# A low-part pass of attention logits on all 128 rows instead of 64

## The chip, the cores and the metric

The kernel runs on one core of a Trainium2 chip. The metric is device time in microseconds (us) of one execution; the time before is 652.01 us, the median of three runs (650.62 to 652.3).

The engines are named as the profile names them: PE is TensorE's matmul, PEld its weight load, DVE is VectorE, ACT is ScalarE, POOL is GpSimd, SP is SyncE, which issues most of the transfers. PE, DVE, ACT and POOL each run their own instructions in order and wait for one another by semaphores.

## The reference, cut to what matters

The reference is one encoder layer on 512 tokens of 1024 channels: a mixer (eight state-space heads and eight attention heads side by side), a norm, a mixture of 16 experts of which each token uses two, and a second norm. The change lies in the attention heads. For each head `h` of 64 channels and each block of 128 queries it computes

```python
logits = jnp.einsum('bqhd,bkhd->bhqk', q[:, q0:q1], k[:, :q1]) * scale   # d = 64
logits = logits + fcum[:, :, q0:q1, None] - fcum[:, :, None, :q1]
logits = jnp.where(qpos >= kpos, logits, -jnp.inf)
probs = jax.nn.softmax(logits, axis=-1)
out = jnp.einsum('bhqk,bkhd->bqhd', probs, v[:, :q1])
```

So query block `t` (0 to 3) needs logits against the first 128 (t + 1) keys.

## The kernel before, in words

**Stages.** The first 178 us project the input and run the state-space scans. The attention heads follow, to about 272 us, woven with projections that they do not depend on. Then come the rest of the output projection (to about 303 us), the first norm and the router (to about 326 us), 16 experts, one after the other (to about 618 us), and the last norms.

**Exact products from parts.** PE multiplies numbers of a reduced format (fp32r). The kernel therefore splits each operand into a high part and a low part, whose sum is the number, and leaves out only the product low by low. Usually that takes three passes: high by high, high by low and low by high.

**The parts of q and k.** `qk_proj` (L651) makes these for a pair of heads: `proj_T` (L243) leaves 128 channels by 512 tokens in a PSUM bank of the tag `pj`, which has two banks; rows 0 to 63 belong to the pair's even head and rows 64 to 127 to the odd one. The first round (m = 0) is q, the second (m = 1) is k. For head j of the pair, `own` are its 64 rows and `other` the rows of its neighbour. A tile `both[j]` of 128 rows by 512 columns takes, for q, the high part in `own` (L669, ACT) and the low part in `other` (L672, DVE). For k it takes the high part in both (L669 and L671, ACT). One pass over 128 rows of these two thus adds q high by k high and q low by k high. The low part of k goes to a third tile, `kl` (L672, DVE): both heads of the pair share one tile of 512 columns, each with its own 64 rows. It is cut from a slab of 1024 columns, of which the second half stays unused (L666).

**The logits.** `head_S` (L687) computes one head's block t into a PSUM bank by three passes: L694 over 128 rows (q's tile by k's tile, n = 128 (t + 1) columns), L695 over the 64 rows `rows` (q high by k low, n columns), and L696, which adds the causal mask to the last 128 columns with a bfloat16 identity as weights. Then DVE subtracts and finds the maximum (L700), ACT takes the exponential (L703), and DVE or POOL scale (L705). `head_T` (L707) transposes and splits the probabilities, `head_PV` (L718) multiplies by v, and `head_close` (L728) adds and splits the output. There are 8 heads of 4 blocks, and so 32 calls of `head_S`.

**Order of work.** PE runs strictly in the order in which the program emits its instructions (`MANUAL`, L78). `heads()` (L740) is a generator that yields amounts of time, and `weave` (L866) puts that much work from a second stream, `fill_stream` (L840), between its steps: projections of the next pairs' q and k (L250), then the output projection (L809). The fill runs on when the heads end, until 303 us. The other engines' orders are laid out by a planner from estimated times; instructions may be moved ahead of earlier ones there. The slabs (`U`, L163) are a ring of 31 buffers of 1024 columns, shared by all phases; the expert weights stream into the same ring as it comes free.

**POOL in this stage.** It computes the low parts of weights (L234, L795) and scales the logits of blocks 0 and 1 (L705).

Of the kernel before, what the change touches and what calls it, by code (L numbers as in the profile page):

```python
# [16 lines left out]
P = 128  # L17
# [55 lines left out]
# whose down projections follow an expert's gate and up projections  # L73
DOWN = [[]] + [[e - 1] for e in range(1, NEXP - 3)] + [[NEXP - 4, NEXP - 3], [NEXP - 2], [NEXP - 1]]
# order of the steps of the last norms: of a tile's, or the last expert's
# [7 lines left out]
def hybrid_layer(ctx: ExitStack, tc: tile.TileContext, x, xT, wu, w16, bT, bz, bv, b16, cw, cb,  # L83
# [22 lines left out]
    # ---- constants that depend on shapes alone  # L106
# [10 lines left out]
    # strict[j, l] = 1 where j < l  # L117
# [10 lines left out]
    # -big above the diagonal (column > row), and below it  # L128
# [11 lines left out]
    def rsqrt(o, var, mult, add, eng=V):  # L140
        """o = (var * mult + add) ** -0.5 on [P, n]"""
        eng.tensor_scalar(o, var, mult, add, op0=OP.mult, op1=OP.add)
        G.tensor_tensor(o, o, mhalf[:, : o.shape[1]], op=OP.pow)
# [5 lines left out]
    # tokens' places with each expert (1 and up, 0 for none), and what an expert's list holds  # L149
    # of a token: its number (less BIG) in two parts and its weight in three, exact in bfloat16  # L150
# [8 lines left out]
    # slabs of 4 KB and of 1 KB a partition, shared by all phases  # L159
# [17 lines left out]
    # ---- x^T and the columns of w_in as exact pairs of float32r parts  # L177
# [7 lines left out]
    def first_x(q, n):  # L185
        """x^T of two blocks of channels, in n parts: first the loads, then the splits"""
        xr = U("xr")
        h_, l_ = (wide("x", n, NX) if 2 * q + i < NX else U(n, F32R) for i, n in enumerate(("xh", "xl")))
        for j in range(2):
            xh[2 * q + j], xl[2 * q + j] = h_[:, j * S:(j + 1) * S], l_[:, j * S:(j + 1) * S]  # L190
        src = xT[q * 256:(q + 1) * 256, :].rearrange("(k p) s -> p k s", p=P)
        for j in range(n):
            c_ = slice(j * 1024 // n, (j + 1) * 1024 // n)
            SY.dma_start(xr[:, c_].rearrange("p (k s) -> p k s", s=S), src[:, j * 2 // n:(j + 1) * 2 // n])
            yield
        for j in range(n):
            c_ = slice(j * 1024 // n, (j + 1) * 1024 // n)
            split(h_[:, c_], l_[:, c_], xr[:, c_])
            yield

    def first_w(u, q, n):
        """half of a unit's columns, likewise"""
        wr_ = U(f"wr{u}")
        h_, l_ = wide("wh", f"wh{u}", 4), wide("wl", f"wl{u}", 4)
        units.setdefault(u, []).append([t_.rearrange("p (k c) -> p k c", c=256) for t_ in (h_, l_)])
        for j in range(n):
            c_ = slice(j * 1024 // n, (j + 1) * 1024 // n)
            SY.dma_start(wr_[:, c_].rearrange("p (k c) -> p k c", c=256),
                         wu[u, :, 4 * q + j * 4 // n:4 * q + (j + 1) * 4 // n])
            yield  # L210
        for j in range(n):
            c_ = slice(j * 1024 // n, (j + 1) * 1024 // n)
            A.activation(h_[:, c_], wr_[:, c_], AF.Copy)
            for d_ in (slice(c_.start, c_.start + 512), slice(c_.start + 512, c_.stop)):
                if d_.start < c_.stop:
                    G.tensor_tensor(l_[:, d_], wr_[:, d_], h_[:, d_].bitcast(F32), op=OP.subtract)
            yield
# [23 lines left out]
    # The tensor engine runs in the order of emission. Work is written as generators that  # L241
    # yield the tensor engine's microseconds, so that independent streams can be woven.
    def proj_T(u, m, r):  # L243
        """r gets out[channel, token] of 128 channels of a unit"""
        pt = bank("pj", "pjT")
        i = 0
        for k in range(KC):
            h_, l_ = units[u][k // 4]
            for w_, x_ in ((h_, xh), (h_, xl), (l_, xh)):
                T.matmul(pt, lhsT=w_[:, k % 4, m * P:(m + 1) * P], rhs=x_[k], start=(i == 0), stop=(i == 23))  # L250
                i += 1
            yield 0.64
        r.append(pt)

    def proj_T2(u, r):
        """both halves of a unit together, block by block as these arrive"""
# [10 lines left out]
    def proj_R(u, t, r):  # L267
        """r gets out[token, 256 channels] for one tile of tokens"""
# [10 lines left out]
    # ---- the first loads, in the order of their use  # L279
# [9 lines left out]
    # ---- per-channel parameters  # L289
# [17 lines left out]
    # rows (chunk, head) of a 64-row table: which head, which chunk  # L307
# [3 lines left out]
    # triones[j, l] = 1 where j <= l  # L311
# [16 lines left out]
    # bias of the convolution's input: what all four taps add, and what the first  # L328
    # three tokens lack of it
# [16 lines left out]
    # ---- dt and the forget gates: [token, tile, (dt 8 | f 8)]  # L346
# [8 lines left out]
    def gates():  # L355
# [15 lines left out]
        # softplus(v) = max(v, 0) + log1p(exp(-|v|)); log1p(e) = 2 atanh(e / (2 + e))  # L371
# [13 lines left out]
        # decays: da = dt * a, a = -exp(a_log)  # L385
        V.scalar_tensor_tensor(da, sp[:, :, 0:8], -1.0, an[:, None, :].to_broadcast([P, NT, 8]), op0=OP.mult, op1=OP.mult)
        V.tensor_scalar(dth, sp[:, :, 0:8], 0.5, None, op0=OP.mult)
        # 8 log f of head h on 16 copies each
# [5 lines left out]
        # cumulative sums within 128-token chunks, and their totals  # L394
# [8 lines left out]
        # rows -8 F[s]: partition (a, h) holds head h  # L403
# [8 lines left out]
        # the chunks' cumulative sums as rows (chunk, head), spread over a group's heads  # L412
# [13 lines left out]
    # ---- state-space heads, one group of four heads at a time  # L426
# [6 lines left out]
    def conv2(in_, blk):  # L433
        """2 silu(conv(proj + bias)) of 128 channels: [channel, token]"""
# [12 lines left out]
    def tt4(o, a, sc4, op, eng=V):  # L447
        """o[p, 256] = a[p, 256] op sc4[p, head]"""
# [8 lines left out]
    def prep(g):  # L457
        """projections, convolution and operands of a group's scan"""
# [37 lines left out]
        # hi and lo parts side by side, so that one pass serves both  # L496
# [35 lines left out]
    def scan(g):  # L532
        """yields the time that the tensor engine may be given to other work"""
# [8 lines left out]
        def decay(c):  # L542
            # decay matrix times C B^T: [s, (head, l)]
# [27 lines left out]
        for c in range(NT):  # L571
# [37 lines left out]
            # 2 silu(z) y, normed over the group's channels  # L609
# [18 lines left out]
    # ---- attention  # L628
    # (a head's hi and lo parts of v lie side by side, and those of its q one over the other,
    # so that one pass serves both)  # L630
# [20 lines left out]
    def qk_proj(pr):  # L651
# [3 lines left out]
        for m in range(2):  # L655
# [10 lines left out]
            kl = halves("kl")[0] if m else None  # L666
            for j in range(2):
# [4 lines left out]
                V.scalar_tensor_tensor(kl[own] if m else both[j][other], pt[own], bcol[own], both[j][own].bitcast(F32),  # L672
# [14 lines left out]
    def head_S(hd, t):  # L687
        q_, k_, kl = qk[hd // 2]
        q_, k_ = q_[hd % 2], k_[hd % 2]
        rows = slice((hd % 2) * HD, (hd % 2 + 1) * HD)  # L690
# [4 lines left out]
        T.matmul(sc[:, :n], lhsT=q_[rows, tq], rhs=kl[rows, :n], start=False, stop=False)  # L695
        T.matmul(sc[:, tq], lhsT=identb, rhs=maskq, start=False, stop=True)  # L696
        # -logits, and minus their maximum
# [42 lines left out]
    def heads():  # L740
        """yields the time that the tensor engine may be given to other work"""
# [42 lines left out]
    # ---- output projection; the state-space half of it fills the end of the attention  # L784
# [32 lines left out]
    # ---- router on rows u before their norm: logits = rs (u g wr - mu 1 g wr) + (b wr + br)  # L817
# [19 lines left out]
    # ---- weaving  # L837
# [54 lines left out]
    # ---- expert weights stream in from here on  # L892
    raw = {}

    def pieces():
        """the experts' weights in the order of their use: (expert, piece)"""
# [32 lines left out]
    # ---- experts  # L929

    def seats_of(pool, place_, eng):
        """[token, seat] of an expert: 1 where the token has the seat"""
# [6 lines left out]
    def list_of(pool, se, entry_, tokens=True, weights=True):  # L939
        """numbers of the tokens in 128 seats (I32), and their weights"""  # L940
# [52 lines left out]
    def gate_up(e, xt_, tag="pj"):  # L993
        """r gets the activations; yields after pairs of pieces"""
# [62 lines left out]
    # ---- second norm: in steps that may be woven  # L1057
    def stats(pool, halves_):
        """mean and variance of rows given as two halves"""
# [6 lines left out]
    def final(pool, u, t, o, junk, eng=V, st=V):  # L1066
        """a tile's rows, normed: with statistics from the engine st"""
# [20 lines left out]
    def final_last(u, ul):  # L1088
        """the last expert's tokens, normed"""
# [17 lines left out]
    def ln2_rows():  # L1107
        """the second norm's gain and bias on all partitions: a half of one at each step"""
# [14 lines left out]
    # ---- first norm, router  # L1123
# [5 lines left out]
    # what column i must exceed column j by, or equal, to come before it in order of size: nothing if  # L1129
    # i < j, the least number if i > j; and i = j never does  # L1130
# [92 lines left out]
    def rows_(t_):  # L1223
        """[p, tile, row, column] as [p, (tile, row), column]"""
# [4 lines left out]
    def choose(t0, t1):  # L1229
        """groups and experts of some tiles' tokens"""  # L1230
# [4 lines left out]
        # rows of four: the groups, and each group's experts; how many columns come before each  # L1235
# [10 lines left out]
    def seat():  # L1246
        """tokens' places: how many before them chose the expert, plus one"""
# [7 lines left out]
    def weigh():  # L1255
        """weights of the two: w0 = 1 / (sum exp (g - max)) / (1 + exp(l1 - l0)), w1 = w0 exp(l1 - l0); over alpha"""
# [97 lines left out]
    # tokens of each expert  # L1354
# [35 lines left out]
    # all tokens are finished without the last expert's product, and its tokens then redone  # L1390
# [31 lines left out]
    # ---- tokens beyond the first 128 of an expert  # L1422
    cnt = nc.values_load(cnt_i[0:1, 0:1], min_val=0, max_val=S, skip_runtime_bounds_check_because="at most every token")
    with tc.If(cnt > P):
        with tc.tile_pool(name="ov", bufs=1) as ov:
            # (and the last expert's first 128, whose products the sums above took from PSUM)
# [108 lines left out]
```

## Time and profile before

| | before |
|---|---|
| median of three runs | 652.01 us |
| range of the runs | 650.62 to 652.3 us |
| span of the profiled execution | 649.7 us |
| PE busy | 586.1 us (90%) |
| DVE busy | 529.2 us (81%) |
| ACT busy | 415.5 us (64%) |
| POOL busy | 248.7 us (38%) |
| PE's share of the chain that ended last | 62% |

The span runs from the first to the last instruction of one profiled execution; no other time is recorded for that execution. The three timed runs lie 0.9 to 2.6 us above it. A busy share is an average over stages; the chain of work that ended last says which engine set the time at each moment. In the chain, a piece's time is only its part of the chain, from its release to the next piece's, so that overlapping passes are not counted twice. In the timeline, a pass's duration includes the time for which it overlaps the next one.

### The profile page before, as it was taken

The numbers are of one execution on the slowest core, as the hardware profiler recorded it, in microseconds if no ns is written. First come the engines' busy times: TensorE is split into PE (matmuls) and PEld (weight loads), VectorE is DVE, ScalarE is ACT, GpSimd is POOL, SyncE is SP. The second block draws the span as 40 slices with busy tenths as digits, with TensorE's granted clock in tenths as the row PEclk, the third lists the DMA queues.
The fourth block names the chain that finished last, engine by engine and source line by source line (L and its number), as shares of the span: only waits on it lengthen the run. The fifth ranks groups of instructions, "written<-read, shape, count | busy, mean of one in ns | idle before, by whom it ended". The sixth has DMA issues, their size and how long they took to land.

```text
span 649.7 us, 9097 instructions
## 1 busy us (share of the span) xinstructions
PE 586.1 (90%) x3007; PEld 477.0 (73%) x3007; DVE 529.2 (81%) x869; ACT 415.5 (64%) x629; POOL 248.7 (38%) x248
## 2 busy tenths in 40 slices
PE   5888996999999999999398999999999999999950
PEld 4677786888776767788277888888888888877830
DVE  3986789688658797765879999999999999999673
ACT  5443353443577875523267888888888888887770
POOL 6537623733452341015614223333333322310282
PEclk9897997999999999998589999999999999999985
DMA  8421122211111174994888999999999999992342
GB/s 263 137 74 54 65 66 66 82 66 64 66 66 45 47 238 134 369 370 165 307 293 307 320 371 358 382 361 352 346 350 341 366 343 361 322 361 55 115 176 83
DMA packets 61702, 141.39 MB, mean 218 GB/s; under 512 B 9987, under 2 KB 10003, under 8 KB 61648
## 3 DMA queue, kind: packets, MB, share of 16 engines
q1 hardware_dynamic: 55168, 125.79, 54.1%
q0 software_dynamic: 5904, 12.85, 7.1%
q10 hardware_dynamic: 576, 2.10, 0.8%
q8 instruction: 25, 0.41, 0.3%
q14 instruction: 29, 0.24, 0.1%
HBM read 134.69 MB, written 14.68 MB: 230 GB/s over the span
## 4 chain that ended last, share of the span: by engine, by line
PE 62%; DVE 13%; ACT 6%; issue 6%; DMA 6%; POOL 5%; SPq 0%; POOLq 0%; ACTq 0%; DVEq 0%
PE pw L809 6%; PE pg L1003 5%; PE pg L1005 4%; PE pg L1004 4%; PE py L1037 4%; PE pu L1003 4%; PE pu L1005 4%; PE pu L1004 4%; PE py L1039 4%; PE py L1038 4%; PE pjT L250 4%; PE pjR L274 3%; DVE acc L437 3%; PE pxg L979 2%; DMA wr<-in_wu 1%
## 5 line engine op out<-in xcount | busy, mean ns | idle before, releaser
L986 ACT ACTIVATE eh<-wf 128x1024 fp32r<-128x1024 f32 x192 | 203.1, 1061 | 49.8 <-PE pg L1005 15.2
L234 POOL TENSOR_TENSOR wl<-wr,wh 128x512 fp32r<-128x512 f32 x40 | 57.0, 1449 | 45.0 <-ACT wh L229 42.2
L957 POOL DMA_INDIRECT xg<-hb,ix x16 | 21.1, 1317 | 112.7 <-PE pg L1005 107.5
L1043 POOL DMA_INDIRECT ub<-yo,ix x15 | 27.2, 1811 | 88.7 <-ACT at L103 54.4
L1037 PE MATMUL py<-eh,at 128*128 128x512 f32 x128 | 52.5, 410 | 2.7 <-ACT at L103 2.5
L1003 PE MATMUL pg<-eh,xgh 128*128 128x512 f32 x128 | 53.1, 415 | 0.8 <-ACT xgh L103 0.8
L1039 PE MATMUL py<-eh,at 128*128 128x512 f32 x128 | 50.9, 398 | 0.0
L1005 PE MATMUL pg<-eh,xgl 128*128 128x512 f32 x128 | 50.7, 396 | 0.0
L1003 PE MATMUL pu<-eh,xgh 128*128 128x512 f32 x128 | 50.0, 391 | 0.0
L1005 PE MATMUL pu<-eh,xgl 128*128 128x512 f32 x128 | 49.9, 390 | 0.0
L250 PE MATMUL pjT<-xh,wh 128*128 128x512 f32 x112 | 46.3, 413 | 1.6 <-DVE kl L672 1.6
L274 PE MATMUL pjR<-wh,xh 128*128 128x256 f32 x128 | 39.3, 307 | 8.6 <-ACT acc L429 7.6
L250 PE MATMUL pjT<-xh,wl 128*128 128x512 f32 x112 | 44.1, 394 | 0.0
L250 PE MATMUL pjT<-xl,wh 128*128 128x512 f32 x112 | 43.9, 392 | 0.0
L936 POOL TENSOR_SCALAR se<-seats,place 128x128 bf16<-128x128 f32 x56 | 43.5, 792 | 0.5
L274 PE MATMUL pjR<-wl,xh 128*128 128x256 f32 x128 | 38.1, 298 | 0.0
L274 PE MATMUL pjR<-wh,xl 128*128 128x256 f32 x128 | 38.0, 297 | 0.0
L274 PEld LDWEIGHTS pjR<-wh,xh 128*128 128x128 f32 x128 | 26.3, 206 | 9.3 <-ACT acc L429 8.0
L1037 PEld LDWEIGHTS py<-eh,at 128*128 128x128 f32 x128 | 24.5, 191 | 8.6 <-ACT at L103 2.7
L1005 PEld LDWEIGHTS pg<-eh,xgl 128*128 128x128 f32 x128 | 24.3, 190 | 6.1 <-DVE xgl L104 0.8
L1039 PEld LDWEIGHTS py<-eh,at 128*128 128x128 f32 x128 | 24.4, 191 | 5.9 <-DVE at L104 0.8
L1003 PEld LDWEIGHTS pg<-eh,xgh 128*128 128x128 f32 x128 | 24.3, 190 | 5.0 <-ACT xgh L103 1.2
(951 smaller groups left out, 1757.7 us busy)
## 6 DMA issues: line engine op xcount, KB each, us to landing
wf<-in_w_up SPq DMA_DIRECT2D x64, 512.0 KB
wf<-in_w_gate SPq DMA_DIRECT2D x64, 512.0 KB
wf<-in_w_down SPq DMA_DIRECT2D x60, 512.0 KB
wr<-in_wu SPq DMA_DIRECT2D x22, 512.0 KB
wor<-in_w_out SPq DMA_DIRECT2D x8, 512.0 KB
hh<-in_x SPq DMA_DIRECT2D x4, 512.0 KB
wf<-in_w_down POOLq DMA_DIRECT2D x4, 512.0 KB, 7.9
u<-ub SPq DMA_DIRECT2D x4, 512.0 KB
```

What stands on the lines that cost most here:

```text
L234: G.tensor_tensor(l_[:, j], wr_[:, j], h_[:, j].bitcast(F32), op=OP.subtract)
L250: T.matmul(pt, lhsT=w_[:, k % 4, m * P:(m + 1) * P], rhs=x_[k], start=(i == 0), stop=(i == 23))
L274: T.matmul(pt, lhsT=x_[k][:, t * P:(t + 1) * P], rhs=w_[:, k % 4, :], start=(i == 0), stop=(i == 23))
L809: T.matmul(pw, lhsT=m_[k][:, ts_], rhs=wo[k][w_][:, c_], start=(i == 0), stop=(i == 11))
L936: eng.tensor_scalar(r[t], seats, place_(t), None, op0=OP.is_equal)
L986: A.activation(h_, src, AF.Copy)
L1003: T.matmul(pt, lhsT=h_[:, k], rhs=wh_[:, f], start=(k == 0), stop=False)
L1004: T.matmul(pt, lhsT=h_[:, k], rhs=wl_[:, f], start=False, stop=False)
L1005: T.matmul(pt, lhsT=l_[:, k], rhs=wh_[:, f], start=False, stop=(k == KC - 1))
L1037: T.matmul(pt, lhsT=h_[:, f], rhs=wh_[:, c_], start=(f == 0), stop=False)
L1039: T.matmul(pt, lhsT=l_[:, f], rhs=wh_[:, c_], start=False, stop=(f == 3))
L1043: G.indirect_dma_start(out=ub, out_offset=bass.IndirectOffsetOnAxis(ap=ix, axis=0), in_=yo, in_offset=None, bounds_check=S - 1, oob_is_err ...
```

## The change

The tile `kl` becomes two, one for each head of the pair, in the two halves of the slab that was taken before too. In each, the head's `own` rows take the low part of k as before, and POOL writes zeros to the `other` rows. The second pass of `head_S` then uses all 128 rows of q's tile and of `kl[j]`: the rows of q low are multiplied by zeros. The rest of the diff removes comments, and moves no other instruction.

```diff
@@ qk_proj
-            kl = halves("kl")[0] if m else None
+            kl = halves("kl") if m else None
             for j in range(2):
                 own, other = slice(j * HD, (j + 1) * HD), slice((1 - j) * HD, (2 - j) * HD)
                 A.activation(both[j][own], pt[own], AF.Identity, bias=bcol[own])
                 if m:
                     A.activation(both[j][other], pt[own], AF.Identity, bias=bcol[own])
-                V.scalar_tensor_tensor(kl[own] if m else both[j][other], pt[own], bcol[own], both[j][own].bitcast(F32),
+                    G.memset(kl[j][other].bitcast(F32), 0.0)
+                V.scalar_tensor_tensor(kl[j][own] if m else both[j][other], pt[own], bcol[own], both[j][own].bitcast(F32),
                                        op0=OP.add, op1=OP.subtract)
@@ head_S
-        q_, k_ = q_[hd % 2], k_[hd % 2]
-        rows = slice((hd % 2) * HD, (hd % 2 + 1) * HD)
+        q_, k_, kl = q_[hd % 2], k_[hd % 2], kl[hd % 2]
...
         T.matmul(sc[:, :n], lhsT=q_[:, tq], rhs=k_[:, :n], start=True, stop=False)
-        T.matmul(sc[:, :n], lhsT=q_[rows, tq], rhs=kl[rows, :n], start=False, stop=False)
+        T.matmul(sc[:, :n], lhsT=q_[:, tq], rhs=kl[:, :n], start=False, stop=False)
         T.matmul(sc[:, tq], lhsT=identb, rhs=maskq, start=False, stop=True)
```

## Rows read from the trace of the kernel before

**Rows 1.** The page's head and its first part: busy us, share, instructions.

```profile
span 649.7 us, 9097 instructions
PE 586.1 (90%) x3007; PEld 477.0 (73%) x3007; DVE 529.2 (81%) x869; ACT 415.5 (64%) x629; POOL 248.7 (38%) x248
```

**Rows 2.** Stretches: PE, PEld, DVE, ACT, POOL busy (instructions), clock, DMA share, GB/s.

```profile
178.00:272.00 94.00, 91.02 (x452) 66.66 (x450) 68.76 (x183) 65.29 (x144) 29.08 (x27) 1.00 0.40 138
222.00:233.00 11.00, 10.95 (x56) 8.10 (x55) 8.45 (x21) 9.87 (x19) 6.89 (x4) 1.00 0.42 132
...
450.00:500.00 50.00, 50.00 (x249) 41.13 (x248) 47.97 (x59) 41.97 (x52) 17.44 (x16) 1.00 0.98 346
```

**Rows 3.** Line L695: idle us of PEld before it, times.

```profile
  issue: 7.9, 32
```

**Rows 4.** Chain that ended last, 257 to 273 us: start, us, piece.

```profile
257.02 0.06 PE sc L694
257.08 0.25 PE sc L695
257.33 0.16 PE sc L696
257.49 0.75 PE pw L809 x3
258.24 0.12 PE sc L694
258.36 0.31 PE sc L695
...
259.27 0.70 PE pw L809 x3
...
260.31 0.18 PE sc L694
260.48 0.36 PE sc L695
...
263.95 0.23 PE sc L694
264.18 0.43 PE sc L695
264.61 0.18 PE sc L696
...
271.74 0.41 PE po L725 x4
```

**Rows 5.** Timeline of PE, 64 to 65 us: start, duration, instruction.

```profile
64.21 0.73 PE L547 MATMUL pl<-RL,csel 64*128 64x512 f32 x2
64.87 0.39 PE L548 MATMUL pl<-maskl,identb 128*128 128x512 bf16 x1
```

**Rows 6.** POOL by line and form: busy us, mean ns.

```profile
L322 POOL MEMSET cself<- 64x512 f32 x1 | 0.5, 523 | 0.0
```

**Rows 7.** Timeline of POOL and PE, 170 to 182 us; brackets: idle before, releaser.

```profile
170.79 2.73 POOL L234 TENSOR_TENSOR wl<-wr,wh 128x512 fp32r<-128x512 f32 x2
...
175.38 0.47 PE L250 MATMUL pjT<-xh,wh 128*128 128x512 f32 x1 [1.58 <-DVE kl L672]
...
179.35 2.55 POOL L234 TENSOR_TENSOR wl<-wr,wh 128x512 fp32r<-128x512 f32 x2 [5.83 <-ACT wh L229]
```

**Rows 8.** Chain that ended last, 196 to 238 us, parts not on PE.

```profile
199.34 0.09 ACT lg L703
...
201.34 2.51 DVE m L104
...
205.04 0.50 PE po L725
...
218.63 0.69 DVE lg L700
...
236.09 0.77 DVE kl L672
```

## The prediction

> **What bounds the kernel now.** I read the page's shares first [rows 1]: PE is busy 90% of the span, DVE 81%, ACT 64%. Such averages do not price one stage, so I went to the stretch of the attention heads [rows 2]. Of its 94.0 us PE is busy 91.0, DVE 68.8 (73%), ACT 65.3 (69%) and POOL 29.1 (31%), at a granted clock of 1.00, the upper level of 2.4 GHz. PE has 3.0 us of idle time there, so what it saves should move the end, unless another engine is the limit in some part. Whether one is, the chain of waits tells, below.
>
> Next I looked at the pass that changes. Ahead of L695 the weight load sat idle 7.9 us in 32 times, 0.25 us each, and for nothing that a semaphore shows ("issue") [rows 3]. So the weights of the 64-row pass are not loaded while the pass before it runs, as they are elsewhere. The chain of one head's four calls shows what that costs [rows 4]. L694, over 128 rows, takes 0.06, 0.12, 0.18 and 0.23 us of the chain for 128, 256, 384 and 512 columns. L695, over 64 rows and as many columns, takes 0.25, 0.31, 0.36 and 0.43: a nearly constant 0.18 to 0.20 more. The same excess stands at the only other 64-row pair [rows 5]: two L547 passes of 512 columns start at 64.21 and the next pass at 64.87, 0.66 us for both. Plain passes of 512 columns take 0.23 (0.70 for three at 259.27 [rows 4]), and 0.66 is 0.23 + 0.43. So two 64-row passes in a row pay the excess once: it belongs to leaving that form, and not to the pass.
>
> **The change part by part.** *The 32 passes (PE).* Before, in the chain, with the mask pass L696 and what the three plain passes behind take beyond 0.70 (0.75 at 257.49, so 0.05) [rows 4]: 128 columns 0.06 + 0.25 + 0.16 + 0.05 = 0.52; 256 columns 0.12 + 0.31 + 0.16 = 0.59 (transposes follow; the 0.16 of L696 repeats for 256 and 384); 384 columns 0.18 + 0.36 + 0.16 + 0.05 = 0.75; 512 columns 0.23 + 0.43 + 0.18 + 0.05 = 0.89.
>
> After, L695 is a pass as L694 is. The price of a short one comes from four plain passes at the end of the heads, two of 256 columns and two of 128, 0.41 us in all [rows 4]: 0.12 + 0.12 leaves 0.17 for the two short ones, 0.06 and 0.11, the second held up by the next weights. So 128 columns: 0.11 + 0.06 and 0.12 for the mask pass with the load behind it, 0.29. 256 columns: 0.12 + 0.12 + 0.07 = 0.31. 384 columns: 0.18 + 0.18 + 0.12 = 0.48. 512 columns: 0.23 + 0.23 + 0.12 = 0.58. The saving is 0.23 + 0.28 + 0.27 + 0.31 = 1.09 us a head, 8.7 us for eight. From below: if only L695 itself becomes plain and the mask pass keeps its price, 0.14 + 0.19 + 0.18 + 0.20 = 0.71 a head, 5.7 us. From above, the mask pass at 0.06 and nothing behind it: 0.06 more in three of the four calls, 10.2 us. I take 8.7, since the idle weight loads of [rows 3], 7.9 us, and some idle ahead of the mask's weights agree with it.
>
> The Trainium skill speaks against this. "TensorE: Matmul & The Clock Gate", section "LDWEIGHTS (loading the stationary operand)", has the time of a weight load depend on the columns alone, so that a load of few rows takes as long as one of 128. By that rule the row count would be worth nothing, and the sum 0. The same skill, in "TensorEngine Tiling (Array Packing)", section "Key Properties", says that a change of the tiling mode drains the engine. By that one the excess goes with the mode. The trace sides with the second: 0.43 against 0.23 us for the same columns [rows 4], and 0.66 for two in one mode [rows 5].
>
> *Eight memsets (POOL).* The nearest row is a memset of the same shape, 0.523 us [rows 6]; 8 make 4.2 us. POOL is idle 65 of the 94 us [rows 2], and nothing has to be read, so that a memset can run as soon as its slab is free. With that cover it costs nothing; from above, if each stood in front of the chain, 4.2 us. I take 0, since kl of the first pair is ready at about 175.4, and the program lets L695 read it only after the projections and the head's opening; POOL has an idle stretch of 5.8 us just then, before 179.35 [rows 7].
>
> *The added wait.* L695 now waits for DVE and POOL. PE is in order, so everything of both streams stands behind it; it costs nothing while the zeros are ready before the low part. If the planner makes the DVE step of `kl` wait for the memset as well, behind it on DVE stand the softmax steps, and the PSUM bank that PE needs for its next projection: PE waited 1.58 us for exactly that release at 175.38 [rows 7]. Between 0 and the price of the slower rival below I take 0, as the two instructions write different rows.
>
> *What is late next.* Two parts of the heads' chain do not run on PE [rows 8]. From 199.34 to 205.04 it runs over ACT and DVE, with one subtraction of 2.51 us on DVE. From 218.63 to 236.09 it runs over ACT, POOL, a load of output weights and ACT again; ACT is busy 9.87 of 11 us there [rows 2]. What PE saves inside these stretches it then waits. A head lasts about (264.18 - 218.4) / 4 = 11.4 us (the last call of head 7 [rows 4] against that of head 3, just before DVE's 218.63 [rows 8]), so that 5.7 + 17.5 = 23.2 us hold two heads' worth of calls: 2.0 x 1.09 = 2.2 us lost. Between 0 lost (these stretches begin earlier and also get shorter) and 4.4 (twice as much), I take 2.2.
>
> *Behind the heads.* The output projection is PE's to 303 us and starts earlier. The norm and the router are a chain of latencies that moves as a whole. The experts keep PE busy 50.00 of 50 us [rows 2], so they end earlier by as much. Their weights are a stream of 0.98 DMA share; a lead of 6.5 us asks for 6.5 x 346 = 2.2 MB, some four or five slabs, sooner, and the heads free their slabs sooner by about the same time.
>
> *Sum.* 8.7 - 2.2 = 6.5 us. Against the profiled span: 649.7 - 6.5 = 643.2. The median of the runs stands 2.3 us above that span, and I leave the distance: 652.0 - 6.5 = 645.5 us.
>
> **The rivals.**
> *All of it is kept.* If the ACT stretches start earlier by what PE gained before and have slack, 8.7 us come through: 643.3. For it: ACT is busy only 69% over the stage. Against: it is nearly full just where the chain lies on it.
>
> *Another engine takes over.* With PE at 91.0 - 8.7 = 82.3 us, DVE's 68.8 and ACT's 65.3 come close, both wait on one another within each head, and new estimates may change the planner's order on ACT and DVE. Then only 2 to 4.5 us are left, 648.8 in the middle.
>
> *Nothing moves.* Either the row count is not the cause, as the skill's first rule would have it, or the weights' stream sets the end of the experts whatever comes before: 652.0. For the latter: a DMA share of 0.98. Against: PE does not pause in those 50 us, and it is PE that would wait if the stream were late.
>
> *Slower: the zeros hold up the low part of k.* The place is L672 at m = 1, once for each pair. If the dependence is kept for a tile and not for its rows, DVE's step waits for the memset, the memset for its turn on POOL behind the weight parts of the next unit, two of them 2.73 us at 170.79 [rows 7], and the second memset again for the first step on DVE: 2.73 + 2 x 0.52 = 3.8 us at worst for a pair, 15 for four. From 6.5 / 4 = 1.6 us a pair on it eats the gain; at 3 us a pair the time is 652.0 - 6.5 + 12 = 657.5. For it: PE already waits for `kl` at 175.38 [rows 7], and the chain passes through `kl` at 236.09 [rows 8]. Against: a memset reads nothing, and POOL has room.
>
> **How the numbers follow.** Forecast (645.5, its own range 643.8 to 647.5): 0.52. All kept: 0.15. Another engine takes over: 0.16. Nothing moves: 0.08. Slower: 0.09. The range leaves out the slower case, half of the unmoved one and the lower tail of the first rival: 642.6 to 651.5. 0.3%, 2.0 us, is about what a measurement of this kernel can tell from no change; by that, faster 0.82 (0.52 + 0.15 + most of 0.16), same 0.09, slower 0.09.
>
> **What would show it.** Right: L695's rows read 128*128; no "issue" idle stands ahead of its weight loads; in the chain a 512-column L695 takes 0.23; the last call of the heads starts 6 to 7 us earlier, and every expert starts earlier by the same. The loss would show as longer waits of PE at the passes behind 205 and 236 us, for DVE and ACT. Wrong: L695 keeps 0.43 (then rows are not the cause); POOL's memsets stand behind a weight part, and PE or DVE wait for them; or the heads end earlier but PE begins to wait within the experts for weights. The forecast is wrong on its size if PE's new waits in the heads add up to more than 5 us or less than 1.

## The result, and the profile after

| | before | changed |
|---|---|---|
| median | 652.15 us (650.62 to 652.45, 4 runs) | 646.05 us (645.41 to 646.51, 4 runs) |
| profiled execution | span 649.7 us | 646.35 us, span 644.3 us |
| heads: head 0's opening to the last mask pass | 178.34 to 264.54 us, 86.2 | 177.54 to 258.66 us, 81.1 |

The ratio of the times is 0.9909, with a 95% interval of 0.9886 to 0.9933: 6.1 us faster, and between 4.4 and 7.4. The forecast was 645.5 us.

In the changed kernel the lines have moved a little: the three passes of `head_S` are L695, L696 (the low part of k) and L697 (the mask), the memset is L673, the low part of k L674, the transposes are L716, the products with v L726, the output projection is L810, and its weights' low part L796. The page's head and first part answer to [rows 1] (busy us, share, instructions):

```profile
span 644.3 us, 9107 instructions
PE 577.7 (90%) x3007; PEld 476.5 (74%) x3007; DVE 529.4 (82%) x869; ACT 415.0 (64%) x629; POOL 252.7 (39%) x256
```

PE has as many instructions as before and is busy 586.1 - 577.7 = 8.4 us less; POOL has eight more instructions and 4.0 us more. The span is only 5.4 us shorter. The stretches, in the columns of [rows 2]:

```profile
178.00:266.00 88.00, 82.51 (x447) 65.12 (x445) 69.46 (x183) 64.18 (x144) 32.28 (x33) 1.00 0.44 146
222.00:233.00 11.00, 8.94 (x45) 6.30 (x43) 9.73 (x19) 9.03 (x18) 7.10 (x6) 1.00 0.71 239
450.00:500.00 50.00, 50.00 (x249) 41.13 (x248) 47.96 (x60) 42.17 (x52) 17.15 (x17) 1.00 0.98 348
214.00:235.00 21.00, 18.61 (x100) 14.17 (x99) 17.10 (x39) 18.00 (x36) 10.88 (x8) 1.00 0.46 151
```

In the heads PE is now idle 88.00 - 82.51 = 5.5 us, where it was idle 3.0 [rows 2]. Of the eleven microseconds from 222 it leaves 2.06 unused, where it left 0.05. In the experts nothing has changed: PE is full, and DMA has the same share. Next the line of the low part by itself, answering to [rows 3] (duration ns, least, median and most; first and last start; shapes):

```profile
L696 PEld LDWEIGHTS sc<-kl,qk x32: 187/188/192, 179.5 to 258.2; 128*128 128x128 f32 x32
L696 PE MATMUL sc<-kl,qk x32: 273/307/397, 179.5 to 258.4; 128*128 128x128 f32 x8, 128*128 128x256 f32 x8, 128*128 128x384 f32 x8, 128*128 128x512 f32 x8
its engine sat idle before it (us, times) until:
who waited for it (us, times):
```

Nothing stands under the idle time: the 7.9 us of issue are gone. The timeline of head 7's call of 512 columns (start, duration, instruction; in brackets idle before, releaser) shows where they stood, in the lines of PE and PEld. First the kernel before:

```profile
263.79 0.40 PE L694 MATMUL sc<-qk 128*128 128x512 f32 x1
264.11 0.18 PEld L695 LDWEIGHTS sc<-kl,qk 64*128 64x128 f32 x1 [0.36 <-issue]
264.11 0.50 PE L695 MATMUL sc<-kl,qk 64*128 64x512 f32 x1
...
264.54 0.23 PE L696 MATMUL sc<-maskq,identb 128*128 128x128 bf16 x1
```

Then the changed kernel:

```profile
258.19 0.40 PE L695 MATMUL sc<-qk 128*128 128x512 f32 x1
258.19 0.19 PEld L696 LDWEIGHTS sc<-kl,qk 128*128 128x128 f32 x1
258.42 0.40 PE L696 MATMUL sc<-kl,qk 128*128 128x512 f32 x1
...
258.66 0.23 PE L697 MATMUL sc<-maskq,identb 128*128 128x128 bf16 x1
```

The weights are now loaded at 258.19, a whole pass ahead, where the load stood until 264.11 before. From start to start, the pass ahead took 0.32 us and the 64-row pass 0.43; they take 0.23 and 0.24 now. So the form cost 0.09 on the way in and 0.19 on the way out. The chain of waits within head 1 (start, us, piece) gives the prices that answer to [rows 4]:

```profile
186.32 0.12 PE sc L695
186.44 0.12 PE sc L696
186.56 0.07 PE sc L697
186.63 0.37 PE ptr L716 x3
187.00 0.02 issue
187.02 0.33 PE ptr L716
```

L696 now takes what L695 takes, 0.12 us for 256 columns (the other calls, not shown, have 0.06 and 0.11 for 128 columns, twice 0.18 for 384 and twice 0.23 for 512), and the mask pass behind it 0.07 in place of 0.16. The four transposes after the second call are what went the other way. They took 0.44 us before and take 0.37 + 0.02 + 0.33 = 0.72: PE comes to the fourth one before DVE has scaled its block. DVE's timeline there (start, duration, instruction) shows what DVE was doing:

```profile
184.26 1.46 DVE L706 TENSOR_SCALAR lg<-lg,rs 128x384 f32<-128x384 f32 x1
...
186.48 0.49 DVE L706 TENSOR_SCALAR lg<-lg,rs 128x512 f32<-128x512 f32 x1
```

The scaling of 384 columns took 1.46 us, most of it beside a weight part on POOL (182.94 to 185.48). In the kernel before, the same scaling came at 186.13, after POOL's weight part had ended at 185.89, and took 0.44, although POOL ran a scaling beside it. The block that PE waits for was then ready at 187.82, 1.0 us before the transposes began (188.83); now it is ready at 186.97, and they begin at 186.47. Over the heads, the eight scalings of 384 columns take 695 ns on the mean, against 496 before.

PE's waits for other engines within the heads (engine, line, what it waited for: us in total, times, longest), 177 to 267 us:

```profile
PE po L726 <- DVE pl L104: 1.6, 1, 1.6
PE ptr L716 <- DVE lg L706: 1.2, 2, 0.7
PE po L726 <- DVE plq L104: 0.9, 1, 0.9
PE pw L810 <- DVE kl L674: 0.7, 1, 0.7
PE prq L832 <- DVE rq L829: 0.6, 1, 0.6
PE ptr L716 <- DVE pl L104: 0.4, 2, 0.2
```

These are 5.4 us in all. In the kernel before, the same answer over the heads has four lines of 1.0, 0.7, 0.7 and 0.5 us: po for DVE's pl, ptr for lg, pw for kl, prq for rq, 2.9 in all. The listed waits have grown by 2.5 us, all of it at DVE, as much as the idle time of the stretches. The chain where it leaves PE, answering to [rows 8]:

```profile
198.52 2.47 DVE m L104
...
203.59 1.06 ACT woh L795
...
209.19 0.76 DVE kl L674
```

It is off PE at the places of before, and also in between, from 203.59 to 213.20, where ACT copies output weights, makes the next q and k and takes exponentials. Last, POOL's timeline (start, duration, instruction), answering to [rows 7]:

```profile
170.43 1.09 POOL L673 MEMSET kl<- 64x512 f32 x2
171.49 2.51 POOL L234 TENSOR_TENSOR wl<-wr,wh 128x512 fp32r<-128x512 f32 x2
```

The two memsets of the first pair ran ahead of the weight parts and not behind them. Each took 0.52 us, and in all eight cases nobody waited for them, though a scaling of 384 columns on DVE that ran beside one took 0.76 us in place of 0.42 (at 202.70, and likewise at 206.23 with the zeros alone below). They did one thing that was not foreseen: they pushed the weight part behind a step of DVE that it had run beside. DVE's timeline there, in the kernel before (first line) and in the changed one:

```profile
170.87 1.50 DVE L616 SCALAR_TENSOR_TENSOR zs<-zs,rst,g_bz 128x256 f32<-128x256 f32 x1 [0.97 <-POOL rst L143]
170.40 0.48 DVE L616 SCALAR_TENSOR_TENSOR zs<-zs,rst,g_bz 128x256 f32<-128x256 f32 x1 [0.97 <-POOL rst L143]
```

`kl` follows on DVE, and PE's wait for it ahead of the heads, 1.58 us in [rows 7], is 1.25 now. Of the fourteen executions in this document, the three without memsets have 1.50 for this step and 1.58 or 1.59 for the wait. The eleven with them have 0.48 or 0.49, and waits of 1.25 to 1.27, but for the two that clear more rows (1.39 and 0.67).

**Where the time went, head by head.** I take the time from one head's opening (`pfb`) to the next one's. For head 7 the end is the start of its last mask pass. From head 0 to head 7 the gains are 1.07, 0.71, 0.56, 0.71, -0.22, 0.22, 0.94 and 1.09 us, 5.1 in sum. What a head saves without its waits is read from its four calls, each from the start of its first pass to the start of what follows its mask pass: head 7's took 0.44, 0.59, 0.76 and 0.79 us, and take 0.21, 0.30, 0.47 and 0.51. That is 1.09 less, and heads 0 and 7 bring all of it through. Eight times that is 8.7, near the 8.4 by which PE's busy time fell. Against 1.09 a head, heads 4 and 5 lost 2.2 us, head 2 lost 0.5, heads 1 and 3 lost 0.8 (0.28 of it at the transposes above), head 6 lost 0.1, and heads 0 and 7 nothing: 3.6 in all. The rest of the profiled difference lies outside the heads. The changed kernel's execution reached them 0.8 us sooner, 0.3 of it by the shorter wait for `kl`, and took 0.5 us longer behind them: 0.8 + 5.1 - 0.5 = 5.4. That start moved from 177.5 to 180.4 us over the executions below, in no order of their edits.

### The profile page after: what moved, and what is told of

Its sections match the earlier page's. It is cut to its first block, busy times and chain, and to the rows that moved or that the text cites. A ratio compares the mean times of both kernels' runs of the same rounds, so it can differ in the third digit from the quotient of the medians.

```text
span 644.3 us, 9107 instructions
## 1 busy us (share of the span) xinstructions
PE 577.7 (90%) x3007; PEld 476.5 (74%) x3007; DVE 529.4 (82%) x869; ACT 415.0 (64%) x629; POOL 252.7 (39%) x256
## 4 chain that ended last, share of the span: by engine, by line
PE 57%; DVE 15%; ACT 8%; DMA 7%; issue 6%; POOL 5%; SPq 0%; POOLq 0%; ACTq 0%; DVEq 0%
PE pw L810 6%; PE pg L1004 5%; PE pg L1006 4%; PE pg L1005 4%; PE py L1038 4%; PE pu L1004 4%; PE pu L1006 4%; PE pu L1005 4%; PE py L1040 4%; PE py L1039 4%; PE pjT L250 3%; DVE acc L437 3%; DMA wr<-in_wu 2%; PE pxg L980 2%; POOL wl L234 1%
```

## The experiments

In the expectations, A is the account of the prediction: the 64-row form costs its excess once when PE leaves it, the memsets cost nothing, and what is lost is lost where DVE and ACT set the pace, in heads 2 to 5. The other letters are rivals, each named in its text.

**Zeros alone.** The changed kernel, but the pass takes the head's own 64 rows again.

```diff
-        T.matmul(sc[:, :n], lhsT=q_[:, tq], rhs=kl[:, :n], start=False, stop=False)
+        rows = slice((hd % 2) * HD, (hd % 2 + 1) * HD)
+        T.matmul(sc[:, :n], lhsT=q_[rows, tq], rhs=kl[rows, :n], start=False, stop=False)
```

> The two tiles and the eight memsets of the change are kept, but the second pass again reads only the head's own 64 rows. Theory A (the time comes from the pass leaving the 64-row form): 652.1, as before, within 1 us; the memsets cost nothing. Rival B (the separate tiles or the planner's new order bring it): 646 to 649. Rival C (the memsets cost something that the change's gain hides): 653 to 656.

Measured: 651.97 us against 652.08, ratio 0.999 [0.9977, 1.0003]; heads 86.3 us. The line of the pass, in the trace of this kernel (there L697; columns as above):

```profile
L697 PE MATMUL sc<-kl,qk x32: 322/408/500, 181.1 to 265.0; 64*128 64x128 f32 x8, 64*128 64x256 f32 x8, 64*128 64x384 f32 x8, 64*128 64x512 f32 x8
...
  issue: 7.9, 32
```

The idle of [rows 3] is back to the tenth. The interval leaves between 1.5 us of gain and 0.2 of loss for the two tiles and the eight memsets, and the trace shows 0.3 of gain ahead of the heads (PE's wait for `kl` is 1.26 us here too). The gain in the heads is the form of the pass. Which 64 rows it uses makes no difference: in the kernel before, the call of 512 columns took 0.79 us in head 6 (rows 0 to 63) and in head 7 (rows 64 to 127).

**The 64-row pass twice.** The kernel before, with its second pass issued twice.

```diff
         T.matmul(sc[:, :n], lhsT=q_[rows, tq], rhs=kl[rows, :n], start=False, stop=False)
+        T.matmul(sc[:, :n], lhsT=q_[rows, tq], rhs=kl[rows, :n], start=False, stop=False)
```

> The kernel before, with its 64-row pass issued twice in a row (the low part of k is added twice). Theory A (the excess is paid once, on going into and out of the form): the second pass costs a plain one, 0.11 + 0.12 + 0.18 + 0.23 = 0.64 us a head, 5.1 us in all, less a fifth for the stretches that do not run on PE: +4 us, 656. Rival B (each 64-row pass pays for itself, 0.25 + 0.31 + 0.36 + 0.43 = 1.35 us a head, 10.8 in all, less a fifth): +8.6 us, 660.7.

Measured: 657.79 us, ratio 1.0095 [1.0069, 1.0121], 5.7 us more. PE's timeline in this kernel, one call of 512 columns (start, duration, instruction):

```profile
259.12 0.40 PE L694 MATMUL sc<-qk 128*128 128x512 f32 x1
259.44 0.49 PE L695 MATMUL sc<-kl,qk 64*128 64x512 f32 x1
259.78 0.39 PE L696 MATMUL sc<-kl,qk 64*128 64x512 f32 x1
260.10 0.23 PE L697 MATMUL sc<-maskq,identb 128*128 128x128 bf16 x1
```

From the first of the two to the mask pass it is 260.10 - 259.44 = 0.66 us, where one alone takes 0.43 [rows 4]: the second adds 0.23, a plain pass's price. For the shorter calls it adds 0.11, 0.12 and 0.18, so 0.64 a head and 5.1 for eight. That is A's price, and a price per pass would be 10.8. The time by itself decides less: 5.7 us, with an interval of 4.5 to 7.9, lies between A's 4 and B's 8.6 and excludes both. In the profiled execution the heads are 7.3 us longer, but the granted clock was 0.50 from 240.3 to 243.7 us, within the heads, where that of the kernel before was 1.00. So the rows show it: what 64 rows cost above 128 is paid once for a run of such passes.

**The 128-row pass twice.** The changed kernel, with its second pass issued twice.

```diff
         T.matmul(sc[:, :n], lhsT=q_[:, tq], rhs=kl[:, :n], start=False, stop=False)
+        T.matmul(sc[:, :n], lhsT=q_[:, tq], rhs=kl[:, :n], start=False, stop=False)
```

> The changed kernel with its 128-row pass issued twice (the low part of k is added twice). Theory A: the added pass costs a plain one, 0.11 + 0.12 + 0.18 + 0.23 = 0.64 us a head, as the added 64-row pass did (0.11 + 0.13 + 0.19 + 0.23 in its timeline), and PE's waits in the heads, 5.4 us, take up part of it: +3 to +5 us on the changed kernel, 649 to 651. Rival B (a pass over all rows with zeros in half of them is dearer than one over 64): more than 652.1.

Measured: 652.81 us, ratio 1.0003 [0.9983, 1.0024], against 652.24 of before. This is above what A gave, and where B put it. PE's timeline in this kernel:

```profile
253.38 0.39 PE L695 MATMUL sc<-qk 128*128 128x512 f32 x1
253.60 0.39 PE L696 MATMUL sc<-kl,qk 128*128 128x512 f32 x1
253.83 0.39 PE L697 MATMUL sc<-kl,qk 128*128 128x512 f32 x1
254.06 0.23 PE L698 MATMUL sc<-maskq,identb 128*128 128x128 bf16 x1
```

The price is plain: 0.22, 0.23 and 0.23 us between starts. With 0.11, 0.12 and 0.17 for the shorter calls that is 0.63 a head, 5.0 for eight, and the heads of the profiled execution are 4.6 us longer than the changed kernel's. The runs show 652.81 - 646.05 = 6.8 us. In the profile 1.5 of the difference lies ahead of the heads (179.08 against 177.54), where this edit adds nothing, and its ten runs spread from 649.54 to 655.39. So the rows bear A's price out; the time by itself does not.

**Only some pairs.** The changed kernel, with the 64-row pass kept for pairs 1 and 2 (heads 2 to 5), and then the reverse, with it kept for pairs 0 and 3.

```diff
-        T.matmul(sc[:, :n], lhsT=q_[:, tq], rhs=kl[:, :n], start=False, stop=False)
+        rows = slice((hd % 2) * HD, (hd % 2 + 1) * HD) if hd // 2 in (1, 2) else slice(0, P)
+        T.matmul(sc[:, :n], lhsT=q_[rows, tq], rhs=kl[rows, :n], start=False, stop=False)
```

In the second kernel the list reads `(0, 3)`.

> The change, with 128 rows only for the heads of pairs 0 and 3 (heads 0, 1, 6 and 7); heads 2 to 5 use 64 rows. Theory A (the part that is lost is lost where the chain runs over ACT and DVE, within heads 2 to 5): these four heads keep all, 4 x 1.09 = 4.4 us, 647.7. Rival B (every head loses its share because DVE and ACT come close everywhere): half of the 6.1 us, 649.1.

> The complement: 128 rows only for heads 2 to 5. Theory A: 4.4 us less the 2.4 us of PE's longer waits, about 2 us or less, 650.2 to 651.5. Rival B: half of the 6.1 us, 649.1.

Measured: the change in pairs 0 and 3 alone gives 646.59 us, ratio 0.991 [0.9891, 0.993], and heads shorter by 3.9 us. In pairs 1 and 2 alone it gives 649.64, ratio 0.9965 [0.9949, 0.9981], and heads shorter by 1.2. Together that is 5.1, the heads' gain of the whole change. PE's waits in the heads of the first of these kernels:

```profile
PE po L727 <- DVE pl L104: 1.0, 1, 1.0
PE ptr L717 <- DVE lg L707: 0.8, 2, 0.5
...
```

With the two that are left out (0.7 and 0.5), these are the waits of the kernel before, to a tenth. The second kernel has the six lines of the changed one, number for number. So the new waits come from saving PE time in heads 2 to 5, where 1.2 of some 4.4 us (four heads at 1.09) get through. Of the other four heads' 4.4 us, 3.9 get through, not all as A had it: head 1 loses 0.4 without them too. In the medians the split is 5.5 and 2.4, whose sum, 7.9, exceeds the 6.1 of the whole; no loss can be read from that sum, and the place of the loss rests on the traces.

**The zeros in the way.** The changed kernel, but POOL clears all 128 rows, so that DVE's step has to wait for it.

```diff
-                    G.memset(kl[j][other].bitcast(F32), 0.0)
+                    G.memset(kl[j].bitcast(F32), 0.0)
```

> The changed kernel, but POOL writes zeros to all 128 rows of each new tile, so that the DVE step that writes the low part must wait for POOL. Theory A (the memsets run as soon as the slab is free, ahead of the low part): 646, within 1 us of the change. Rival C (a wait of DVE on POOL here costs 1.6 us or more a pair, since kl is on the chain at 175 and 236 us): 650 to 657.

Measured: 645.46 us, ratio 0.9892 [0.9868, 0.9917]; the memset takes 0.524 us, as for 64 rows. DVE's waits ahead of `kl` in this kernel, in the columns of PE's waits above:

```profile
DVE kl L674 <- ACT qk L672: 2.1, 3, 0.7
...
DVE kl L674 <- POOL wl L234: 1.2, 1, 1.2
```

In the changed kernel these are 2.8 us for ACT in four waits, the longest 1.1, and none for POOL. So with the dependence that the slower rival needs, one wait of 1.1 has turned into one of 1.2, in the first pair and ahead of the heads, and the time is no longer than the changed kernel's. The profile puts that wait to the weight part that runs behind the memsets and ended at 174.89 us, 0.07 after ACT's copy; the memsets themselves had ended at 172.40. A wait of DVE on POOL thus comes up, and has next to no price here: the memsets come early enough.

**Output weights later.** The changed kernel, with the last four output weights issued after blocks 1 and 2 and not after each block, to clear ACT and POOL in heads 4 and 5.

```diff
-            load_wo(4 + t)
+            if t in (1, 2):
+                load_wo(2 * t + 2)
+                load_wo(2 * t + 3)
```

> The changed kernel with the loads and splits of the last four blocks of the output weights emitted later: two after the second tile of the first half of the output projection, two after the third. Theory A (what is lost of the gain is lost because ACT, DVE and POOL split these weights between 217 and 230 us, long before they are due): PE's waits in the heads fall from 5.4 us by 2 us or more, 643 to 644.5. Rival D (the chain of the heads' own steps is what PE waits for): waits and time stay, 646. Against both: if the splits now come too late or collide with the norm, 647 or more.

Measured: 645.61 us, ratio 0.9893 [0.9869, 0.9917], with PE's waits as in the changed kernel. It tells nothing on its question. ACT's copies started at 218.68, 220.65, 225.53, 226.92 and 229.26 us, about a microsecond from the 217.69, 219.66, 224.69, 226.08 and 228.42 of the changed kernel: the planner moved them ahead again.

**Low parts of the output weights on DVE.** The changed kernel without POOL's share of L796; then the same edit on the kernel before; then on the changed kernel for the first weight alone.

```diff
-WO_G = (0, 2, 4, 6)
+WO_G = ()
```

In the third kernel the list reads `(2, 4, 6)`.

> The changed kernel with all low parts of the output weights computed on DVE (1.22 us each) and none on POOL (2.4 us each, four). Theory F (PE's longer waits in heads 2 to 5 come from DVE steps that stand still while such a POOL step runs: 2.47 us for a subtraction of 0.68, 1.25 and 1.87 for a scaling of 0.45): without them PE's waits in the heads fall from 5.4 us to 3 or less, 643.5 to 644.5. Rival G (DVE is full there, 9.7 of 11 us, and four more steps on it cost what they free): 646 or more.

> The same edit in the kernel before. Theory F: PE has 3.0 us of waits in the heads there, of which 1.7 are of this kind: 650.5 to 651.5, and the difference to the changed kernel with the same edit is 7 us or more. Rival G: 652 or more, with a difference of 6.

> The changed kernel with only the first of these low parts (the one at 198 us) on DVE. Theory F: the wait of 1.6 us of PE for pl at 202 us goes, and the others stay: 644.5 to 645. Rival G: the wait stays or moves, 646.

Measured, against 651.38 of before on that chip: 645.4 us, ratio 0.9901 [0.9877, 0.9926]; 649.96, ratio 0.9971 [0.9954, 0.9987]; and 644.9, ratio 0.99 [0.9875, 0.9925]. The heads take 79.7, 85.1 and 79.9 us. PE's waits and the stretch from 214 to 235 us in the first of these:

```profile
PE po L726 <- ACT ph L103: 1.0, 1, 1.0
...
```

```profile
214.00:235.00 21.00, 18.96 (x102) 14.71 (x101) 18.39 (x43) 18.41 (x37) 2.57 (x4) 1.00 0.44 149
```

POOL's work there falls from 10.88 to 2.57 us and DVE's rises from 17.10 to 18.39; DVE's subtraction for `m`, 2.47 us in the chain above, takes 0.68. PE's waits fall from 5.4 to 4.0 us, and the largest is now for ACT. The heads are 1.4 us shorter, but the time is not distinguishable from the changed kernel's. With this edit on both sides the change is worth 649.96 - 645.4 = 4.6 us, where F asked for 7 or more, and 5.4 in the heads. Of 8.7 saved, 3.3 are still lost: by these executions POOL's share of the output weights makes 0.3 of the change's loss of 3.6, and not the bulk of it. In the third kernel the wait of 1.6 us is gone, as F had it, but one of 0.6 for ACT's `fb` has come in its place.

**ACT's copies on POOL.** The edit before, with five of ACT's copies of output weights moved to POOL too (`WOH_G = (2, 3, 4, 5, 6)`).

> The changed kernel with the low parts of all output weights on DVE, as in the last trial, and the high parts of blocks 2 to 6 on POOL, where ACT spends 1.06 us each, between 217 and 230 us. Theory H (with POOL's long steps gone, ACT is what heads 4 and 5 wait for: it is busy 18.4 of the 21 us from 214 to 235): PE's waits in the heads fall from 4.0 us by 1.5 or more, 643.5 to 644.5. Rival G (DVE is as full as ACT, 18.4 of 21, and POOL's copies hold it up again): 645.4 or more.

Measured: 645.7 us against 651.86, ratio 0.9892 [0.9872, 0.9912]; heads 79.4. The same stretch in this kernel:

```profile
214.00:235.00 21.00, 19.84 (x110) 15.66 (x109) 19.18 (x46) 14.47 (x34) 10.83 (x11) 1.00 0.40 128
```

ACT falls from 18.41 to 14.47 us of the 21, and PE comes up to 19.84; but DVE stands at 19.18, and of PE's 3.8 us of waits 3.2 are for DVE. H asked for 1.5 us less waiting and is not borne out. All versions from 644.9 to 646.05 lie within one another's intervals; none is shown to beat the changed kernel.

**The other 64-row passes.** The changed kernel, with the decay passes of [rows 5] on 128 rows too: `csel` and `cself` keep all rows, and POOL clears the rows above 64 of the operands.

```diff
+                G.memset(o_[64:].bitcast(F32), 0.0)
...
-                T.matmul(pl, lhsT=csel[:, c], rhs=RL[g][i][:64], start=(i == 0), stop=False)
+                T.matmul(pl, lhsT=csel[:, c], rhs=RL[g][i], start=(i == 0), stop=False)
```

> The changed kernel, and the same done to the other 64-row passes: the two passes of each of the 8 decay steps of the scans run on 128 rows, with zeros from 4 further memsets on POOL. Theory A (an excess of 0.2 to 0.3 us for each time that the form is left): 8 x 0.3 = 2.4 us less PE time, of which at least half counts, since PE is busy 85 to 90% in the scans: 643.5 to 645. Rival: the scans wait for DVE there, so that nothing moves: 646.

Measured: 647.46 us, ratio 0.9926 [0.9899, 0.9953]. PE's timeline in this kernel:

```profile
71.26 0.63 PE L548 MATMUL pl<-RL,csel 128*128 128x512 f32 x2
71.73 0.39 PE L549 MATMUL pl<-maskl,identb 128*128 128x512 bf16 x1
```

The pair takes 0.47 us in place of 0.66, two plain passes, and the pass ahead of it 0.09 less too: some 0.28 a pair, 2.2 for eight. The time does not show this gain, and the trace does not say whether it would arrive. PE starts the first pair 0.69 us later than in the changed kernel's execution (64.16 against 63.47) and the seventh 0.03 later (136.60 against 136.57). Then the granted clock falls. The stretch in this kernel and in the changed one (second line), in the columns of [rows 2]:

```profile
145.60:152.40 6.80, 6.80 (x31) 6.19 (x31) 4.14 (x12) 0.92 (x3) 0.00 (x0) 0.50 0.01 2
145.60:152.40 6.80, 6.80 (x55) 6.28 (x54) 5.41 (x15) 2.88 (x9) 0.55 (x1) 1.00 0.00 0
```

At a clock of 0.50, the lower level of 1.2 GHz, PE gets through 31 instructions in place of 55, and the eighth pair starts 2.49 us later (150.37 against 147.88). The three of its seven runs with the lowest mean clock, 0.946 to 0.950, are among the four slowest, and the changed kernel's four runs have 0.953 to 0.956. What lowered the clock was not tested. PE also waits for other engines in the scans (7.5 us for ACT's `acc` alone), with and without this edit.

## Why the prediction was right, step by step

*The 32 passes.* 1.09 us a head was forecast from [rows 4], and head 7's calls gave 1.09, 8.7 us for eight. The cause holds as well: it is the form and not the zeros (zeros alone), and it is paid once for each run of passes (the two 64-row passes). Two readings were less exact. The excess was put to leaving the form; the timeline shows a third of it on the way in, where the pass ahead took 0.32 us in place of 0.23. And the idle time ahead of the mask's weights, which was taken as support, had nothing to do with it: it is 3.4 us in 16 times before and after. The rule that a load's time goes by its columns alone, which the Trainium skill has in "TensorE: Matmul & The Clock Gate", section "LDWEIGHTS (loading the stationary operand)", is true of the load itself, 183 ns with 64 rows against 188 with 128. It misses what these runs price, the 0.25 us for which the load does not start.

*The memsets and the added wait.* Nothing was forecast, and no cost came: 651.97 against 652.08 with the zeros alone. The 0.3 us that they bring ahead of the heads was not foreseen. The reason given, that the two instructions write different rows, proved unnecessary: POOL's zeros come so early that even a real dependence cost no time.

*What is late next.* This is the term that was mis-sized: 2.2 us forecast, 3.6 measured in the heads, within its bounds of 0 to 4.4. The places were right: the heads of the two stretches lost 2.7 us, 0.5 in head 2 and 2.2 in heads 4 and 5. What the step missed lies mostly outside them, 0.9 us in heads 1, 3 and 6. (The 11.4 us of a head there run from one call's third pass to another's second; from like to like they are 11.5, and the two heads' worth stay.) The 0.28 us at head 1's transposes is the plain case, and it is not slack alone: PE's lead moved a scaling on DVE into the time of a weight part on POOL, where it took three times as long. A chain that stays on PE shows that PE is the last, not by how much, nor what a shift will lay over what. PE's new waits, 2.5 us, lie between the 1 and the 5 that were set as the limits of the forecast, but all of them are for DVE, where DVE and ACT were named.

*Behind the heads.* It moved nearly as a whole. The last mask pass came 5.9 us sooner, a little less than the 6 to 7 that were named as the sign, the first pass of expert 0 starts at 321.8 us in place of 327.4, 5.6 sooner, and the span is 5.4 shorter; PE is full from 450 to 500 us as before.

*The sum.* By terms, 8.7 - 3.6 = 5.1 us in the heads, and 0.3 ahead of them, 5.4 where 6.5 were forecast; the medians show 6.1. The two agree within the interval, 4.4 to 7.4. The forecast kept the 2.3 us between the median and the profiled span; in the changed kernel they are 646.05 - 644.3 = 1.7. Apart from the wait for `kl`, the profiled executions differ by half a microsecond at the start of the heads, and by as much, the other way, behind them; such differences between two traces cannot be told from a part of the gain. That 645.5 and 646.05 lie half a microsecond apart is thus partly luck: the loss was 1.4 too low, against 0.3 of gain that was not foreseen and some 0.7 that the medians show and the rows do not.

*What stays open.* Where PE loses 3.6 us, that is mostly in heads 4 and 5, DVE and ACT are both near full (17.10 and 18.00 of 21 us from 214 to 235). Taking work from ACT left DVE full, and taking POOL from DVE's side put the largest wait on ACT. How much each holds was not settled.

## What to carry to other kernels

A short pass in another row form between full ones should be priced by the distance from its start to the next pass's, not by its rows: here 0.43 against 0.23 us, with 0.09 more on the pass ahead of it. Idle "issue" ahead of its weight load was a sign, not a price: the mask pass has such idle time in both kernels. Zeros that fill it up to the full form cost nothing when an idle engine writes them well ahead, and passes that must keep the form are better put next to one another, since the excess comes once. What an engine with 97% of a stage saves does not arrive whole: before summing, look at how far the next engine is from being full in each head, and not only at where the chain already leaves the first.

## What the runs showed of the hardware

- Two 64-row passes of 512 columns took 0.66 us in a row and one took 0.43, and the 128-row pass ahead of them 0.32 in place of 0.23: some 0.29 us of excess per run of them, not per pass. With 128 rows the weights of the low-part pass were loaded beside the pass ahead of it, with no idle at all in 32 cases; of two 64-row passes in a row, the second's weights were loaded beside the first (at 259.55 us, for a pass at 259.78).
- A memset of POOL took 0.52 us for 64 rows by 512 and the same, 0.524, for 128 by 512. A step of DVE on 128x256 took 0.48 us beside two memsets and 1.50 beside a weight part of POOL.
- DVE's subtraction of two 64x512 operands took 2.47 us while POOL ran a subtraction of 128x1024 from 198.05 to 200.44, and 0.68 when POOL's was taken away. DVE's scaling of 384 columns took 1.46 us beside a subtraction of POOL, 0.76 beside a memset, and 0.44 beside a scaling of POOL. The Trainium skill, "SBUF — State Buffer", section "Who interferes with whom", has both kinds of DVE instruction share a pair of ports with POOL, which one of the two holds for a whole instruction; that DVE's subtraction ended 0.55 us after POOL's, about its own length, agrees with it. That the scaling beside POOL's scaling, which had begun 0.24 us before it, was not held up does not.
